# Input projection with convolution and FoX columns first, RWKV columns last, and the recurrence beside the sample's past attention

## The chip, the cores and the metric

The kernel runs on one core of a Trainium2 chip. The metric is the device time of one execution in microseconds (us); of several executions the median is taken. The core has five instruction streams that run in order, each on its own: TensorE (PE, with its weight loads as a row of its own, PEld), VectorE (DVE), ScalarE (ACT), GpSimd (POOL) and SyncE (SP). They wait for each other by semaphores. DMAs are issued from the streams of SP, ACT and POOL, and 16 DMA engines carry them.

## The reference

One inference step of one layer of a hybrid decoder, for a prompt of 512 tokens and for 8 samples of 4 new tokens each, so 544 token columns in all. All arithmetic is float32. Cut to what matters here:

```python
z = rms_norm(x, g_mix) @ w_in               # (544, 1024) @ (1024, 3080)
za, zb, zc = split(z, [1024, 1024 + 1544])  # RWKV | FoX | convolution columns
# RWKV-7: token shift, gates (decay w, a, g), then a recurrence over tokens per head
sa = einsum('bhvk,bhk->bhv', S, -kk_t)
S  = S * w_t + sa[..., None] * (kk_t * a_t) + v_t[..., None] * k_t
# FoX: q, k normed per head, log-sigmoid forget gate, causal attention in the prompt;
# each sample attends to 2048 past tokens from a paged cache and to its own 4
kp = cache_fox_k[l][page_table]; vp = cache_fox_v[l][page_table]
s_past = einsum('bqhd,bkhd->bhqk', q, kp) * scale + cT[..., :, None] + exT[..., None, :]
# convolution: u = a * sigmoid(b), causal depthwise convolution of width 31, layer norm, silu
x = x + concat([ya, yb, yc]) @ w_out
x = x + cross_attend(x, mk, mv, ...)        # mk, mv = projections of 256 memory tokens
x = x + conv_ffn(x, ...)
```

The outputs are x and all new cache rows and states. The past of the samples is 8 x 16 pages of 128 tokens in each of the K and V caches, 67 MB together, which have to be gathered by page number.

## The kernel before

A large product keeps float32 accuracy by splitting both operands: w = w_hi + w_lo and x = x_h + x_l, and taking three passes (`gemm_steps`). For a block of 128 weight columns, ACT casts w_hi from the loaded `w_raw`, DVE subtracts to get w_lo, and PE takes 8 row blocks x 3 passes x 2 spans of token columns = 48 matmuls into a bank `bank_g`, of which there are two. The bank is then evacuated by DVE (`evac_z`, `evac_conv`, `evac_fl`, `evac_fox`). The weights of two blocks are loaded at a time into a ring of two 1 MB buffers called `w_raw`.

The program is written for a tile scheduler: Python generators give their work in steps, `weave` and `woven` take from several of them in proportion to a rate, and the scheduler then fixes the order on each engine, with `urgent` and `high_priority` as its priorities. Nothing is reordered at run time. The part of the program up to the first residual is this:

- **Start.** The tokens are loaded, transposed and split into `act_h` and `act_l` (`xh`, `xl`); the forget-gate sums of the past (`LF`, `LT`, `later`, `NX`) are made.
- **RWKV columns.** 8 blocks of `w_in` (`order_z`), each followed by the token shift (`evac_z`), with the gates (`gates`) made as soon as the blocks that they need are there.
- **FoX and convolution columns beside the recurrence.** `fox_and_conv` takes one block of forget gates (`evac_fl`), 4 of the convolution (`evac_conv`) and 12 of FoX (`evac_fox`, then `fox_block` with norm, transposes and the stores of the new rows). Woven with it are `rwkv_recurrence` (`inverses`, then per pair of chunks `chain`, `stateless` and `stateful`, then `sample_steps` for the samples) and `conv_ahead`, whose `conv_taps` are the 31 taps as multiply-adds of DVE on tiles `four`, with POOL and ACT taking a fifth of the taps.
- **Past attention of the samples beside the rest.** `sample_past` does for each of the 8 samples 4 gathers of K (1 MB each, into the ring `w_raw`, transposed on DVE into `KT`, then products in `bank_s`), a softmax, 4 gathers of V (into the ring `page` of three, products in `bank_v`) and closing steps in `bank_k`. Gathers are issued by POOL (`four_pages`). Beside it runs `rest`: the attention of the prompt (`attend`, in the three banks `bank_r`), the memory norm and the convolution's layer norm (`side_work`), the projections of the memory (`memory`, products of `xT` in `bank_g`), and the output projection with its residual (`out_prompt`, products of `four` in `bank_g`); `out_sample` closes.

The stage after that begins with the cross attention's query projection, whose products are called `bank_d`, and goes on to the feed-forward network; its code is not touched. The line that sets the last stage's rates is

```python
weave((urgent(sample_past(), 0), 135.0), (rest(), 148.0, 0.06))
```

Of the kernel before, what the change touches and what calls it, by code (L numbers as in the profile page):

```python
# [8 lines left out]
F32 = mybir.dt.float32  # L9
# [145 lines left out]
def hybrid_step(tc, A):  # L155
# [375 lines left out]

    rp = ExitStack()
# [9 lines left out]
    f1s = ExitStack()  # L542
    f1 = pool("f1a", 1, f1s)
    reset = f1.tile([128, NT], F32, name="tap")
    load(out=bf, in_=A["fox_b_f"].rearrange("l h -> h l"))
    nc.scalar.dma_start(out=reset, in_=A["cf"][:, -NT:])
    nc.gpsimd.memset(zb[:, :, 0:1], 0.0)
# [135 lines left out]
    for p4, po in enumerate(QUAD):  # L683
        vts(out=kidx[po], in0=ptb[po, p4::4], scalar1=32, scalar2=CU("lane").bitcast(I32)[po], op0=MUL, op1=ADD)
# [10 lines left out]


    f2 = pool("f2a", 2, f1s)
    nc.vector.memset(e8.bitcast(F32), 0.0)
    nc.gpsimd.memset(cum.bitcast(F32), 0.0)
    for po in QUAD:  # L700
        acopy(e8[po.start: po.start + 8], ident[0:8, 0:8])
    nc.vector.memset(cpad, 0.0)
    nc.gpsimd.memset(U[:, :, : CW - 1], 0.0)
    now, after = {}, []

    def finish(n=1):

        for x in after:
            x[0] -= n
        while after and after[0][0] <= 0:  # L710
            after.pop(0)[1]()

    def evac_fl(ps, i, a):

        if a == 0:
            now["y"] = f2.tile([128, NT], F32, name="fraw")[:8]
        y = now["y"]
        with tc.high_priority():
            vtt(out=halves(y)[a], in0=ps[:8], in1=halves(rs)[a][:8], op=MUL)
        if a == 0:  # L720
            return
        vts(out=y, in0=y, scalar1=bf, scalar2=None, op0=ADD)
        logf = f2.tile([128, NT], F32, name="fsq")[:8]
        e = f2.tile([128, NT], F32, name="ft")[:8]
        act(out=e, in_=y, func=AF.Abs)
        act(out=e, in_=e, func=AF.Exp, scale=-1.0)
        act(out=e, in_=e, func=AF.Ln, bias=ones[:8, 0:1])
        vstt(out=logf, in0=y, scalar=0.0, in1=e, op0=MINO, op1=SUB)
        ccum = f2.tile([128, NT], F32, name="ft")[:8]
        nc.vector.tensor_tensor_scan(out=ccum[:, :SEQ], data0=ones[:8, 0:1].broadcast_to([8, SEQ]), data1=logf[:, :SEQ],  # L730
                                     initial=0.0, op0=MUL, op1=ADD)
        nc.vector.tensor_tensor_scan(out=cpad[:8], data0=C("reset_s")[:8], data1=logf[:, SEQ:],
                                     initial=0.0, op0=MUL, op1=ADD)
        for ro in HALF:
            acopy(cum[ro][:8], ccum[:, :SEQ])
            vtt(out=cum[ro][32:40], in0=ccum[:, :SEQ], in1=cum[0:8].bitcast(F32), op=SUB)
        after.append([6, lambda: fl_rows(logf)])

    def fl_rows(logf):
        ps = xb()  # L740
        for i in range(4):
            tr(ps[:, i * 8: i * 8 + 8], logf[:, i * 128: (i + 1) * 128])
        tr(ps[:NS, 32:40], logf[:, SEQ:])
        lt = f1.tile([128, 40], F32, name="lt")
        vcp(lt[:, :32], ps[:, :32])
        vcp(lt[:NS, 32:], ps[:NS, 32:40])
        store(out=A["p_fox_logf"][0, 0].rearrange("(i p) h -> p i h", p=128), in_=lt[:, :32].rearrange("p (i h) -> p i h", h=8))
        store(out=A["s_fox_logf"][0].rearrange("b t h -> (b t) h"), in_=lt[:NS, 32:])

    def tok_major(dst, dst_s, src, src_s):  # L750

        ps = xb()
        for i in range(4):
            tr(ps[:, i * 128: (i + 1) * 128], src[:, i * 128: (i + 1) * 128])
        anycp(dst, ps.rearrange("p (i c) -> p i c", c=128))
        ps = xb()
        tr(ps[:NS, :128], src_s)
        vcp(dst_s, ps[:NS, :128])

    def evac_fox(ps, i, a):  # L760
        j, kind = i // 3, i % 3
        if a == 0:
            now["raw"] = f2.tile([128, NT], F32, name="fraw")
            if kind < 2:
                now["sq"] = f2.tile([128, NT], F32, name="fsq")
        raw, sq = now["raw"], now.get("sq")
        with tc.high_priority():
            vtt(out=halves(raw)[a], in0=ps, in1=halves(rs)[a], op=MUL)
            if kind < 2:
                act(out=halves(sq)[a], in_=halves(raw)[a], func=AF.Square)  # L770
        finish()
        if a:
            after.append([1, lambda: fox_block(j, kind, raw, sq)])

    def fox_block(j, kind, raw, sq):
        c = slice(j * 128, (j + 1) * 128)
        if kind == 2:
            tok_major(vF[:, :, c], vs[:NS, c], raw[:, :SEQ], raw[:, SEQ:])
            store(out=A["s_fox_v"][0].rearrange("b t h d -> (b t) (h d)")[:, c], in_=vs[:NS, c])
            store(out=A["p_fox_v"][0, 0].rearrange("(i p) h d -> p i (h d)", p=128)[:, :, c], in_=vF[:, :, c])  # L780
            return
        t = f2.tile([128, NT], F32, name="ft")
        sums = []
        for (lo, n) in EVEN:
            ps2 = xb()
            mm(ps2[:, :n], bones, sq[:, lo: lo + n])
            act(out=sq[:, lo: lo + n], in_=ps2[:, :n], func=AF.Ln, scale=1.0 / 64, bias=eps_rms)
            sums.append(ps2[:, :n])
        act(out=sq, in_=sq, func=AF.Exp, scale=-0.5)
        for h in range(2):  # L790
            half_xyy(halves(t)[h], halves(sq)[h], sums[h], 1.0 / 64, EPS_RMS)
        vstt(out=raw, in0=raw, scalar=nkg if kind else qg, in1=sq, op0=MUL, op1=MUL)
        dst, dst_s = ((yF[:, j, :SEQ], qsT[:, j]), (kF[:, j], ksT[:, j]))[kind]
        vstt(out=dst, in0=t[:, :SEQ], scalar=1.5, in1=raw[:, :SEQ], op0=SUB, op1=MUL)
        vstt(out=dst_s, in0=t[:, SEQ:], scalar=1.5, in1=raw[:, SEQ:], op0=SUB, op1=MUL)
        if kind:
# [6 lines left out]
    def evac_conv(ps, i, a):  # L803
        m = i // 2
        finish()
        if i % 2 == 0:
            if a == 0:
                now["a"] = f2.tile([128, NT], F32, name="fraw")
# [1390 lines left out]
```

## Time and profile before

| | |
|---|---|
| median of 3 runs | 1257.33 us (1253.19 to 1261.47) |
| profiled execution | 1253.36 us, of which the span of the trace is 1251.6 us |
| busy PE, PEld, DVE, ACT, POOL | 1162.3, 998.9, 810.1, 499.6, 290.0 us |
| mean granted TensorE clock | 0.965 of full speed |
| DMA | 173.83 MB, mean 139 GB/s |

The span is counted from the first instruction of the trace. Busy time of an engine is the union of its instructions' spans; a matmul's span includes its way through the array, so several overlap and a busy PE need not be at its peak. Idle time is put down to what ended it. A window's row gives its start and end, its length, the busy time of each engine with the number of its instructions (PE, PEld, DVE, ACT and POOL; for a single tile PE, PEld, DVE and ACT, as far as they touch it), then the granted TensorE clock as a share of full speed, the busy share of the DMA engines and what they moved in GB/s. A group's row gives line, engine, operation, output<-input and shapes, the count, and behind the bar the busy time in us, the mean of one in ns, and the idle time just before with what ended it. In the chain and in a timeline the first two numbers are start and length.

### The profile page before, as it was taken

The page shows a single profiled execution, that of the slowest core. Times are in us where ns is not written, and L with a number is a line of the kernel's source. Part 1 is how long each engine was busy: PE and PEld are TensorE (multiplying, and loading weights), DVE is VectorE, ACT ScalarE, POOL GpSimd, SP SyncE. Part 2 cuts the span into 40 slices and gives each one's busy share as a digit, 9 for nine tenths or more (in the row PEclk, how much of TensorE's full clock was granted, in tenths as well). Part 3 has the DMA queues.
Part 4 walks back from the last instruction along what each step waited for, and adds up shares of the span by engine and source line. Part 5 has one row for each costly group of instructions (what it writes and reads, how often), then busy time and mean ns, then how long its engine had stood idle before and what let it go on. Part 6 is the DMA issues. An engine that isn't in the chain of part 4 may idle for free.

```text
span 1251.6 us, 24835 instructions
## 1 busy us (share of the span) xinstructions
PE 1162.3 (93%) x10410; PEld 998.9 (80%) x10410; DVE 810.1 (65%) x1516; ACT 499.6 (40%) x994; POOL 290.0 (23%) x322
## 2 busy tenths in 40 slices
PE   6899989999988998988989979999999999999997
PEld 6788878895654566765478756999999999999996
DVE  4699998865578667772355766567777325767522
ACT  5354453351346554423343233254444223444321
POOL 1253340113533323212322330031111001111120
PEclk9999999998689999989999999999999999999998
DMA  7222220131578799988435361232322332322241
GB/s 236 61 60 51 62 78 2 54 89 44 161 287 323 281 350 360 339 266 277 169 114 160 118 251 59 77 121 70 100 90 59 97 91 95 102 90 70 81 125 36
DMA packets 129649, 173.83 MB, mean 139 GB/s; under 512 B 7029, under 2 KB 110981, under 8 KB 121336
## 3 DMA queue, kind: packets, MB, share of 16 engines
q1 hardware_dynamic: 88160, 70.76, 18.7%
q0 software_dynamic: 15216, 84.80, 18.4%
q10 hardware_dynamic: 26160, 16.66, 4.7%
q8 instruction: 82, 1.34, 0.4%
q14 instruction: 31, 0.25, 0.1%
HBM read 164.54 MB, written 7.88 MB: 138 GB/s over the span
## 4 chain that ended last, share of the span: by engine, by line
PE 65%; DVE 12%; issue 9%; DMA 6%; ACT 5%; POOL 2%; SPq 0%; POOLq 0%; ACTq 0%; DVEq 0%
PE bank_g L186 39%; PE bank_r L186 8%; PE bank_d L186 7%; PE bank_s L186 3%; DMA page<-in_cache_fox_v_dram,kidx 3%; PE bank_a L186 2%; PE bank_v L186 2%; DMA w_raw<-in_cache_fox_k_dram,kidx 2%; DVE KT L1404 2%; DVE w_lo L247 2%; PE bank_r L216 1%; PE bank_t L216 1%; DMA x_tok<-in_x_prompt_dram 1%; PE bank_x L216 1%; ACT w_lo L1440 1%
## 5 line engine op out<-in xcount | busy, mean ns | idle before, releaser
L186 PE MATMUL bank_g<-four,w_hi 128*128 128x272 f32 (+1 forms) x1536 | 277.5, 299 | 5.7 <-ACT w_hi L177 5.0
L177 ACT CAST w_hi<-w_raw 128x1024 fp32r<-128x1024 f32 (+3 forms) x149 | 140.4, 945 | 259.5 <-PE bank_g L186 187.9
L186 PEld LDWEIGHTS bank_g<-four,w_hi 128*128 128x128 f32 x1536 | 221.9, 188 | 15.2 <-ACT w_hi L177 5.3
L247 DVE TENSOR_TENSOR w_lo<-w_raw,w_hi 128x1024 fp32r<-128x1024 f32 (+3 forms) x149 | 163.4, 1098 | 82.4 <-ACT w_hi L177 75.3
L186 PE MATMUL bank_g<-four,w_lo 128*128 128x272 f32 (+1 forms) x768 | 171.8, 299 | 0.0
L186 PE MATMUL bank_g<-act_h,w_hi 128*128 128x272 f32 (+2 forms) x400 | 124.6, 311 | 6.1 <-ACT w_hi L177 2.5
L186 PEld LDWEIGHTS bank_g<-four,w_lo 128*128 128x128 f32 x768 | 122.0, 189 | 5.9 <-issue 3.4
L186 PE MATMUL bank_g<-act_h,w_lo 128*128 128x272 f32 (+2 forms) x400 | 122.5, 307 | 0.0
L186 PE MATMUL bank_g<-act_l,w_hi 128*128 128x272 f32 (+2 forms) x400 | 121.6, 304 | 0.0
L2110 POOL TENSOR_SCALAR ysm<-HS,vec 128x32 f32<-128x32 f32 x44 | 42.0, 954 | 255.1 <-ACT HS L177 255.1
L186 PEld LDWEIGHTS bank_g<-act_h,w_hi 128*128 128x128 f32 x400 | 79.0, 198 | 10.5 <-ACT w_hi L177 2.9
L186 PEld LDWEIGHTS bank_g<-act_h,w_lo 128*128 128x128 f32 x400 | 78.9, 197 | 2.8 <-issue 1.2
L1404 DVE STREAM_TRANSPOSE KT<-w_raw 128x2048 f32<-128x2048 f32 x32 | 73.5, 2301 | 11.7 <-DMA w_raw<-in_cache_fox_k_dram,kidx 10.7
L186 PEld LDWEIGHTS bank_g<-act_l,w_hi 128*128 128x128 f32 x400 | 79.0, 198 | 2.4 <-issue 1.1
L186 PE MATMUL bank_d<-four,w_hi 128*128 128x272 f32 x384 | 78.2, 299 | 0.0
L186 PE MATMUL bank_g<-in_h,w_hi 128*128 128x272 f32 x352 | 73.5, 290 | 0.0
L186 PE MATMUL bank_g<-in_l,w_hi 128*128 128x272 f32 x352 | 73.5, 290 | 0.0
L186 PE MATMUL bank_g<-in_h,w_lo 128*128 128x272 f32 x352 | 73.2, 289 | 0.0
L186 PEld LDWEIGHTS bank_d<-four,w_hi 128*128 128x128 f32 x384 | 61.7, 192 | 1.0
L2102 DVE TENSOR_TENSOR up<-bank_g,tot 128x544 f32<-128x544 f32 x44 | 31.8, 722 | 44.6 <-PE bank_g L186 44.6
L1389 POOL DMA_INDIRECT w_raw<-in_cache_fox_k_dram,kidx x32 | 36.0, 1125 | 94.2 <-DVE KT L1404 62.6
L186 PE MATMUL bank_d<-four,w_lo 128*128 128x272 f32 x192 | 56.7, 295 | 0.0
(632 smaller groups left out, 2439.3 us busy)
## 6 DMA issues: line engine op xcount, KB each, us to landing
w_raw<-in_w_up_dram SPq DMA_DIRECT2D x20, 1024.0 KB, 5.1
w_raw<-in_w_down_dram SPq DMA_DIRECT2D x16, 704.0 KB, 4.5
w_raw<-in_w_in_dram SPq DMA_DIRECT2D x17, 512.0 KB, 4.6
w_raw<-in_cache_mem_k_dram SPq DMA_DIRECT2D x16, 512.0 KB, 5.0
sV<-in_cache_mem_v_dram POOLq DMA_DIRECT2D x12, 512.0 KB, 6.0
w_raw<-in_w_in_dram SPq DMA_DIRECT2D x4, 1024.0 KB, 7.1
w_raw<-in_w_xk_dram ACTq DMA_DIRECT2D x8, 512.0 KB, 12.4
w_raw<-in_w_xv_dram ACTq DMA_DIRECT2D x8, 512.0 KB, 5.1
```

The costliest lines, as they stand in the source:

```text
L177: nc.scalar.copy(out, in_)
L186: pinned(nc.tensor.matmul(out, lhsT, rhs, start=start, stop=stop, skip_group_check=True))
L216: pinned(nc.tensor.transpose(out=out, in_=in_, identity=ident[p0:p0 + k, p0:p0 + k]))
L247: tt(out=l, in0=src, in1=h.bitcast(F32), op=SUB)
L1389: nc.gpsimd.indirect_dma_start(out=t, out_offset=None, in_=A[cache][0].rearrange("n (k j) h d -> (n k) (j h d)", j=4), in_offset=bass.Indi ...
L1404: nc.vector.transpose(out=KT, in_=K)
L1440: anycp(PT[to, j].rearrange("p (g h q) -> p g h q", g=4, q=TS), ps[po].rearrange("p (g h a q) -> p a g h q", g=4, a=4, q=TS)[:, p4])
L2102: vtt(out=two(x[:, 2:]), in0=ev2(ps), in1=two(rstd), op=MUL)
L2110: nc.gpsimd.tensor_scalar(out=ysm, in0=H[:, 2:6, 1:], scalar1=w[2], scalar2=b, op0=MUL, op1=ADD)
```

## The change

Three things are moved, and no arithmetic is added or taken away.

1. The order of the columns of `w_in`. The convolution's 4 blocks are taken first (the preloaded first weights are theirs), then the forget gate and the 12 FoX blocks, woven with `conv_ahead` at rates 106 and 60, and RWKV's 8 blocks last, woven with what is left of `conv_ahead`. The convolution's blocks take spans of 256 and 288 columns now.
2. The recurrence is no longer woven with the projection. It is the first thing in `rest`, so it runs beside `sample_past`; the rate of `rest` goes from 148 to 215, and its head start from 0.06 to 0.03.
3. Pools follow: the FoX pool `f2a` is closed before the RWKV pool `rt` opens, `reset` has a tile of its own, the gather indices `kidx` are made before the RWKV columns, and the pool `cv` is opened only after the recurrence.

```diff
@@ start
-            early = weights(A["w_in"][0], 8, [m * 128 for m in order_z[:2]])
+            early = weights(A["w_in"][0], 8, [COL_CONV, COL_CONV + 256])
...
@@ the block from "f1s, f2s = ExitStack(), ExitStack()" to conv_ahead is moved ahead of the RWKV block, with
+    EARLY = ((0, 256), (256, 288))
+
     def fox_and_conv():
         x = blocks(xh), blocks(xl)
+        yield from gemm_steps(w_in, [COL_CONV + (2 * half + m) * 128 for m in range(2) for half in range(2)], *x, evac_conv, gb,
+                              spans=EARLY, first=early)
+        conv_done[0] = True
         yield from gemm_steps(w_in, [COL_FL], *x, evac_fl, gb)
         for j in range(4):
-            if j == 0:
-                yield from gemm_steps(w_in, [COL_CONV + (2 * half + m) * 128 for m in range(2) for half in range(2)], *x, evac_conv, gb)
-                conv_done[0] = True
             yield from gemm_steps(w_in, [COL_FOX + kind * 512 + j * 128 for kind in range(3)], *x, lambda ps, i, a, j=j: evac_fox(ps, 3 * j + i, a), gb)
         finish(9)
...
+    conv_work = conv_ahead()
+    weave((fox_and_conv(), 106.0), (conv_work, 60.0, 0), first=True)
+    f2s.close()
...
@@ RWKV columns
-    blocks_done, after_r1 = [0], gates()
-    need = next(after_r1)
-    for step in gemm_steps(w_in, [m * 128 for m in order_z], blocks(xh), blocks(xl), evac_z, gb, spans=((0, 256), (256, 288)), first=early):
-        if need is not None and blocks_done[0] >= need:
-            need = next(after_r1, None)
-    for _ in after_r1:
-        pass
+    blocks_done = [0]
+
+    def rwkv_columns():
+        after_r1 = gates()
+        need = next(after_r1)
+        for step in gemm_steps(w_in, [m * 128 for m in order_z], blocks(xh), blocks(xl), evac_z, gb, spans=EARLY):
+            if need is not None and blocks_done[0] >= need:
+                need = next(after_r1, None)
+            yield step
+        for _ in after_r1:
+            pass
+
+    weave((rwkv_columns(), 44.0), (conv_work, 30.0))
...
@@ after the projection
-    recurrence, conv_work = urgent(rwkv_recurrence(), 800), conv_ahead()
-    weave((fox_and_conv(), 106.0), (recurrence, 79.0, 0), (conv_work, 84.0, 0), first=True)
+    recurrence = urgent(rwkv_recurrence(), 800)
...
@@ rest
-        yield from woven((recurrence, 48.0), (conv_work, 48.0))
+        yield from recurrence
         recurrence_end()
...
-    weave((urgent(sample_past(), 0), 135.0), (rest(), 148.0, 0.06))
+    weave((urgent(sample_past(), 0), 135.0), (rest(), 215.0, 0.03))
```

How the order on the engines moves is shown at three places. The first is DVE inside the recurrence's `inverses`, where a small triangular solve goes over 15 steps (`Dr`, then `X`). Before, between its steps stand convolution taps (`four<-U,vec,four`), FoX norms (`ft`, `fraw`) and evacuations:

```order
L955 TENSOR_REDUCE X<-Dr 128x12
L226 SCALAR_TENSOR_TENSOR ft<-bank_x,ft 128x272
L954 TENSOR_TENSOR Dr<-X,zbuf_1206 128x13x13
L794 SCALAR_TENSOR_TENSOR four<-ft,fraw 128x512
L955 TENSOR_REDUCE X<-Dr 128x13
L795 SCALAR_TENSOR_TENSOR qsT<-ft,fraw 128x32
L855 SCALAR_TENSOR_TENSOR four<-U,vec,four 128x512
L768 TENSOR_TENSOR fraw<-bank_g,rs 128x272
L954 TENSOR_TENSOR Dr<-X,zbuf_1206 128x14x14
```

Now, on the same engine in the same solve, transposes of K pages (`KT<-w_raw`) and a sample's softmax (`st`, `Pn`) stand there:

```order
L1416 STREAM_TRANSPOSE KT<-w_raw 128x2048
L968 TENSOR_TENSOR Dr<-X,zbuf_2653 128x11x11
L1435 ISA tq,st<-tq,cf 128x32
L1435 ISA st 128x1
L969 TENSOR_REDUCE X<-Dr 128x11
L1437 RECIPROCAL st<-st 128x1
L968 TENSOR_TENSOR Dr<-X,zbuf_2653 128x12x12
L1439 TENSOR_SCALAR Pn<-Pn,st 128x4
L969 TENSOR_REDUCE X<-Dr 128x12
L1416 STREAM_TRANSPOSE KT<-w_raw 128x2048
```

What fills the gaps of the recurrence on DVE has gone from work whose inputs lie on the chip to transposes that wait for a gather. All 32 K transposes now stand ahead of the last step of the recurrence (`recurrence_end`), the first two of them ahead of `inverses`; of the 32 gathers of V, 19 are issued before it and 13 after.

The second place is PE in the output projection. Before, its products (`bank_g<-four`) alternate with transposes of x and with the last samples' K products:

```order
L186 MATMUL bank_g<-four,w_hi 128x512
L186 MATMUL bank_s<-KT,w_hi 32x128 x32
L216 MATMUL bank_r_6116<-ident,w_raw 128x32 x4
L216 MATMUL bank_r_6122<-ident,w_raw 128x32 x4
L186 MATMUL bank_g<-four,w_hi 128x512
L186 MATMUL bank_g<-four,w_lo 128x512
L186 MATMUL bank_g<-four,w_hi 128x512 x2
L186 MATMUL bank_g<-four,w_lo 128x512
L186 MATMUL bank_g<-four,w_hi 128x512
L186 MATMUL bank_s<-KT,w_hi 32x128 x16
```

Now the memory's and the output's products stand almost alone, as here in the memory's projection on PE:

```order
L186 MATMUL bank_g<-xT_4302,w_hi 128x256
L186 MATMUL bank_g<-xT_4303,w_hi 128x256
L186 MATMUL bank_g<-xT_4302,w_lo 128x256
L186 MATMUL bank_g<-xT_4302,w_hi 128x256
L186 MATMUL bank_g<-xT_4303,w_hi 128x256
L186 MATMUL bank_g<-xT_4302,w_lo 128x256
```

Behind the start of the memory's projection PE has no K product of a sample left, and of V only 16 products and the closing steps.

The third place is SP's queue at the start of the RWKV columns, where the samples' shift state is loaded into the tile `dp`. Now that load stands behind the weights of RWKV's third pair of blocks and waits for six semaphores of POOL's DMA queue (DMASW):

```order
L273 DMA w_raw<-in_w_in_dram 128x8x256 [waits DMAHW4_49,DVE_49]
L273 DMA w_raw<-in_w_in_dram 128x8x256 [waits DMAHW5_49,DVE_49]
L766 DMA dp<-in_state_rwkv_shift_dram 8x512 [waits DMASW2_49,DMASW5_49,DMASW1_49,DMASW6_49,DMASW0_49,DMASW7_49,DVE_49,Activation_49]
L766 DMA dp<-in_state_rwkv_shift_dram 8x512 [waits PE_49]
L273 DMA w_raw<-in_w_in_dram 128x8x256 [waits DMAHW6_49,DVE_49]
```

Before, it waited for no store:

```order
L550 DMA gup<-in_rwkv_g_up_dram 128x256 [waits DMAHW5_49]
L273 DMA w_raw<-in_w_in_dram 128x8x256 [waits DMAHW6_49,DMAHW1_49,DVE_49]
L554 DMA dp<-in_state_rwkv_shift_dram 8x512 [waits DVE_49,DMAHW0_49,PE_49,Activation_49]
L554 DMA dp<-in_state_rwkv_shift_dram 8x512
L273 DMA w_raw<-in_w_in_dram 128x8x128 [waits DMAHW2_49,DVE_49]
```

The load has moved behind the stores of the last FoX rows, whose memory its tile takes over; PE's transposes of `dp` stand among the matmuls of RWKV's second block.

## Rows read from the trace of the kernel before

**Rows 1.** Windows of the whole core

```profile
113.00:320.00 207.00, 199.49 (x2218) 164.05 (x2218) 162.08 (x366) 81.53 (x172) 50.62 (x57) 0.95 0.19 52
320.00:645.00 325.00, 286.77 (x2669) 195.56 (x2667) 210.97 (x404) 145.67 (x356) 97.74 (x90) 0.94 0.78 273
```

**Rows 2.** The same view, shorter windows

```profile
0.00:64.00 64.00, 49.26 (x322) 44.77 (x323) 35.13 (x84) 31.02 (x61) 13.16 (x30) 0.97 0.46 145
64.00:320.00 256.00, 244.05 (x2518) 205.18 (x2517) 210.16 (x432) 105.23 (x203) 74.16 (x76) 0.95 0.20 55
80.00:100.00 20.00, 17.02 (x116) 16.32 (x115) 19.90 (x26) 9.14 (x15) 14.42 (x10) 0.91 0.31 81
120.00:180.00 60.00, 53.25 (x406) 48.93 (x407) 57.21 (x116) 32.23 (x53) 25.47 (x28) 0.97 0.28 73
300.00:320.00 20.00, 20.00 (x62) 9.82 (x62) 5.93 (x19) 2.68 (x8) 1.88 (x2) 0.57 0.11 27
320.00:340.00 20.00, 17.32 (x127) 11.83 (x125) 14.81 (x28) 7.32 (x21) 12.93 (x13) 0.67 0.55 174
323.00:454.00 131.00, 115.41 (x1218) 70.26 (x1216) 96.56 (x201) 70.83 (x206) 49.39 (x50) 0.91 0.79 291
```

**Rows 3.** The chain that ended last: start us, us, what

```profile
46.03 3.40 DMA dp<-in_state_rwkv_shift_dram
338.69 7.58 DMA w_raw<-in_cache_fox_k_dram,kidx
646.93 4.61 PE bank_d L186 x24
```

**Rows 4.** Groups of instructions by line, PE, 13:64

```profile
L186 PE MATMUL bank_g<-act_h,w_hi 128*128 128x256 f32 (+1 forms) x78 | 24.6, 315 | 2.5 <-ACT w_hi L177 2.5
```

**Rows 5.** The same view, DVE, 113:320

```profile
L855 DVE SCALAR_TENSOR_TENSOR four<-U,vec,four 128x512 f32<-128x512 f32 x48 | 38.7, 806 | 0.4
...
L954 DVE TENSOR_TENSOR Dr<-X,zbuf 128x1 f32<-128x1 f32 (+14 forms) x15 | 9.0, 600 | 0.0
...
L1006 DVE COPY_PREDICATED zsb<-cu,bank_r 128x32 f32<-128x32 uint32 x1 | 0.2, 182 | 0.0
```

**Rows 6.** Windows of tile bank_g: PE, PEld, DVE, ACT busy (count), PEclk, DMA, GB/s

```profile
13.00:323.00 310.00, 188.06 (x1200) 165.39 (x1200) 23.11 (x57) 0.00 (x0) 0.96 0.23 63
454.00:540.00 86.00, 54.21 (x384) 50.03 (x384) 6.52 (x16) 2.89 (x8) 0.96 0.97 339
540.00:645.00 105.00, 54.28 (x192) 35.48 (x192) 5.53 (x8) 0.00 (x0) 0.95 0.62 206
```

**Rows 7.** DMA issues, 113:320: KB each, median us from issue to landing

```profile
out_dram<-tok POOLq DMA_DIRECT2D x3, 256.0 KB, 4.5
```

**Rows 8.** Windows of tile bank_r, columns as in rows 6

```profile
113.00:320.00 207.00, 89.41 (x1464) 61.84 (x1463) 35.49 (x99) 18.21 (x47) 0.95 0.19 52
323.00:454.00 131.00, 63.71 (x336) 37.90 (x334) 25.06 (x51) 15.68 (x37) 0.91 0.79 291
```

**Rows 9.** Windows of tile bank_s, then of bank_v

```profile
320.00:645.00 325.00, 51.55 (x1104) 36.02 (x1104) 5.50 (x8) 0.59 (x1) 0.94 0.78 273
...
323.00:454.00 131.00, 20.83 (x128) 5.83 (x128) 0.00 (x0) 1.76 (x3) 0.91 0.79 291
```

**Rows 10.** Groups by line, DVE, 323:454

```profile
L1404 DVE STREAM_TRANSPOSE KT<-w_raw 128x2048 f32<-128x2048 f32 x20 | 45.9, 2298 | 1.1 <-DMA w_raw<-in_cache_fox_k_dram,kidx 1.1
```

**Rows 11.** Timeline of DVE: start us, us, what

```profile
332.96 4.50 DVE L1404 STREAM_TRANSPOSE KT<-w_raw 128x2048 f32<-128x2048 f32 x2
```

**Rows 12.** Tile w_raw on POOL, 330:560: issues' durations in ns, first and last; landing

```profile
L1389 POOL DMA_INDIRECT w_raw<-in_cache_fox_k_dram,kidx x30: 999/1006/2062, 338.7 to 543.7; - x30
...
DMA to landing us min/median/max: 5.5/7.9/11.8
```

**Rows 13.** Timeline of PE at the output projection's first and last products

```profile
550.93 0.80 PE L186 MATMUL bank_g<-four,w_hi 128*128 128x512 f32 x1 [5.05 <-ACT w_hi L177]
...
634.74 0.40 PE L186 MATMUL bank_g<-four,w_lo 128*128 128x512 f32 x1
```

More of the change, by code (lines that the diff above doesn't have):

```diff
@@ L529, in hybrid_step, with finish @@
     gls.close()
+    f1s, f2s = ExitStack(), ExitStack()
+    f1 = pool("f1a", 1, f1s)
+    f2 = pool("f2a", 2, f2s)
+    load(out=bf, in_=A["fox_b_f"].rearrange("l h -> h l"))
+    nc.vector.memset(e8.bitcast(F32), 0.0)
+    nc.gpsimd.memset(cum.bitcast(F32), 0.0)
+    for po in QUAD:
+        acopy(e8[po.start: po.start + 8], ident[0:8, 0:8])
+    nc.vector.memset(cpad, 0.0)
+    nc.gpsimd.memset(U[:, :, : CW - 1], 0.0)
+    now, after = {}, []
+    def finish(n=1):
+        for x in after:
+            x[0] -= n
+        while after and after[0][0] <= 0:
+            after.pop(0)[1]()
@@ new lines, in fl_rows @@
+    def fl_rows(logf):
+        ps = xb()
+        for i in range(4):
+            tr(ps[:, i * 8: i * 8 + 8], logf[:, i * 128: (i + 1) * 128])
+        tr(ps[:NS, 32:40], logf[:, SEQ:])
+        lt = f1.tile([128, 40], F32, name="lt")
+        vcp(lt[:, :32], ps[:, :32])
+        vcp(lt[:NS, 32:], ps[:NS, 32:40])
+        store(out=A["p_fox_logf"][0, 0].rearrange("(i p) h -> p i h", p=128), in_=lt[:, :32].rearrange("p (i h) -> p i h", h=8))
+        store(out=A["s_fox_logf"][0].rearrange("b t h -> (b t) h"), in_=lt[:NS, 32:])
@@ new lines, in tok_major, with evac_fox @@
+    def tok_major(dst, dst_s, src, src_s):
+        ps = xb()
+        for i in range(4):
+            tr(ps[:, i * 128: (i + 1) * 128], src[:, i * 128: (i + 1) * 128])
+        anycp(dst, ps.rearrange("p (i c) -> p i c", c=128))
+        ps = xb()
+        tr(ps[:NS, :128], src_s)
+        vcp(dst_s, ps[:NS, :128])
+    def evac_fox(ps, i, a):
+        j, kind = i // 3, i % 3
+        if a == 0:
+            now["raw"] = f2.tile([128, NT], F32, name="fraw")
+            if kind < 2:
+                now["sq"] = f2.tile([128, NT], F32, name="fsq")
+        raw, sq = now["raw"], now.get("sq")
+        with tc.high_priority():
+            vtt(out=halves(raw)[a], in0=ps, in1=halves(rs)[a], op=MUL)
+            if kind < 2:
+                act(out=halves(sq)[a], in_=halves(raw)[a], func=AF.Square)
+        finish()
+        if a:
+            after.append([1, lambda: fox_block(j, kind, raw, sq)])
@@ L694, in hybrid_step @@
     rp.close()
[L697 to L796, printed above, removed]
-            tokm = f2.tile([128, 4, 128], F32, name="tok", bufs=1)
-            rows = f2.tile([NS, 128], F32, name="krow", bufs=1)
-            tok_major(tokm, rows, dst, dst_s)
-            store(out=A["p_fox_k"][0, 0].rearrange("(i p) h d -> p i (h d)", p=128)[:, :, c], in_=tokm)
-            store(out=A["s_fox_k"][0].rearrange("b t h d -> (b t) (h d)")[:, c], in_=rows)
```

228 lines of the change are left out of this document (139 added, 89 removed).

## Prediction

> **What bounds the kernel now.** I read the windows by stage first: in each, which engine is full, and what it is full of. In the woven stage PE is busy 199.49 of 207 us and DVE 162.08 [rows 1], so neither looks free; but a matmul's span includes its way through the array, and waits of one product for another count as busy. The dense stretches tell more: DVE reaches 19.90 of 20 and 57.21 of 60 us [rows 2]. So where projection, convolution taps and FoX norms meet, DVE is the bound, and PE follows. The end of this stage is different: from 300 to 320 DVE is busy 5.93 of 20 us, PE finishes 62 instructions, and the granted TensorE clock is 0.57 [rows 2]. The recurrence has run dry of filler there, one product waits for the last, and the clock has gone down: (1 - 0.57) x 2 x 20 = 17 us of it at 1.2 instead of 2.4 GHz.
>
> From 323 on the bound is another. The chain goes by gathers of K [rows 3], the DMA engines are 0.79 busy [rows 2], and DVE is at 211 of 325 us [rows 1]. Each K page needs a landing in the ring of two `w_raw`, then a transpose of 2.30 us [rows 10] that empties it. In 454 to 540 the DMA share is 0.97 [rows 6]: the memory's projection shares its weight loads with the gathers.
>
> So the program has a DVE-bound stage with idle DMA (0.19, [rows 1]) and a DMA-bound stage with idle engines. The change lays the recurrence, which needs little DMA, beside the gathers. The section that it touches ends where the cross attention's projection starts, at 646.93 [rows 3]. I sum it anew up to there and leave the rest as it is.
>
> **The change part by part.**
>
> *Start and convolution columns.* By 64 us 232 matmuls of the projection had run (78 + 77 + 77; one of the three rows stands in [rows 4]), a stall for the shift's load included (46.03, 3.40 us, [rows 3]). Now the first 4 blocks and the forget gate's are 240, without that stall: **60 us**.
>
> *The rest of the projection, with all taps and norms.* From 64 to 320 DVE has 210.16 us [rows 2]; what of FoX still came behind 320 I estimate at 10 of the 14.81 us of 320 to 340 [rows 2]. The recurrence's part goes out: in 113 to 320, 47 of the view's 76 groups, from `Dr` with 9.0 us down to 0.2 [rows 5], are its own, 73.9 us of the 182.8 that all groups add up to (their spans overlap), so of the 162.08 us of busy time 65.5. What stays is 210.2 + 10 - 65.5 = 155. At a density of 0.975 (between 57.21/60 and 19.90/20) that is **159 us**. PE's part is 20 blocks x 48 matmuls at 0.141 (54.21/384) to 0.157 (188.06/1200) [rows 6], 135 to 151 us, and some 15 of transposes and small products: just hidden beneath DVE, and not by much.
>
> *The shift's load.* It waits now for stores of the last FoX rows. A store of `tok` took 4.5 us to land [rows 7] and the load 3.40 [rows 3]; PE has a transpose of it among the matmuls of RWKV's second block, so PE's queue stands behind it. The stores may long have landed (bound 0), or nothing covers them (7.9). The weave ends its FoX part just before, so I take **8**.
>
> *The recurrence with the gathers.* All 32 K transposes stand before its last step, the first two ahead of it: 30 pages, and 19 V pages. Four candidates for the bound. DVE: 65.5 of the recurrence, 32 x 2.30 = 73.5 of transposes, and 15 for the softmax of 7 samples, about 155. PE: the recurrence's 89.41 (17 of it at half clock) and 51.55 for K's products, and 19 of 32 V pages, about 30: 165 to 170, [rows 8, 9], of which much is waiting. DMA: 49 MiB at the 339 GB/s of the fullest window [rows 6], 152. The ring: landing 7.9 and transpose 2.3 [rows 10, 12] for two buffers, 5.1 a page, 153. All four stand at 152 to 170, and that is just why none will be met: three rings with queues in fixed order lose at each other. The nearest row of such a mixture is the attention stage: 20 transposes between 332.96 and 454 [rows 10, 11], 6.05 us a page, with DVE at 96.56 of 131 and DMA at 0.79 [rows 2]. At that pace 30 pages are 182, and 6 for the first landing (5.5 at least, [rows 12]): **188 us**. The bounds are 155 and, below, 232.
>
> *Prompt attention with 13 V pages.* Before, `bank_r` held PE for 63.71 us, beside K [rows 8]; 14 V pages cost 20.83 [rows 9]. **84 us**; the gathers themselves, 13.6 MB at 291 GB/s, are 47 and lie beneath.
>
> *Memory's projection.* No gather is left beside it; `bank_g` needs 54.21 us for its 384 matmuls [rows 6] in 86 us of window. **54 us**.
>
> *Head of the output projection.* Its first product waited 5.05 us for ACT's casts [rows 13], and the step before it needs some 3: **8**.
>
> *Output projection.* 192 matmuls held 54.28 us between other work [rows 6]; at the tempo of its last rows, 2 x 0.23 us for 512 columns each, 45. I take **48**.
>
> *Tail.* From its last product, 634.74, to `bank_d`, 646.93 [rows 3, 13]: **12**.
>
> Sum: 60 + 159 + 8 + 188 + 84 + 54 + 8 + 48 + 12 = 621 us, against 646.9: 26 us off the profiled execution's 1253.4, so 1227.5. The median of the runs lies 4 us above the profiled one, half of which I take as belonging to it: **1230 us**.
>
> One rule speaks against this. Gathers are issued by POOL, whose issue took 1.0 us in the median and 2.06 at most [rows 12]; in 323 to 454 DVE was busy three quarters of the time.
>
> The Trainium skill ("SBUF — State Buffer", section "Who interferes with whom") says that VectorE and GpSimd share one pair of ports under an exclusive lock, and that GpSimd can't write the descriptors of a DMA while VectorE holds it. The one stretched issue in the row could be that, and no row shows what it would be beside a VectorE that is never idle. By it each gather would come later, as in the slower case below.
>
> **The rivals.**
>
> *K does not limit.* If landings come down, since the memory's weights no longer share the DMA engines, the stage goes at DVE's 155 + 5 = 160 us, 28 less: 1202. For it: landing at least was 5.5 [rows 12], which gives (5.5 + 2.3)/2 = 3.9 a page. Against it: the median of 7.9 with V beside it, as will be again.
>
> The Trainium skill ("DMA: Bandwidth & Descriptors", section "Anatomy of one DMA — SWDGE (gpsimd) path") fits 2.0 us plus the bytes by 436 GB/s: 4.4 us for a page, an estimate by which K would never limit. The trace disagrees, with 7.9 [rows 12].
>
> *The recurrence's own chain decides.* While it ran before, DVE was idle for 207 - 162.08 = 45 us with all that filler at hand [rows 1], and PE fell to 0.57 clock at its end. If this idle time is the recurrence's latency and comes on top, with the filler now waiting for gathers (some 15 us more), the stage takes 155 + 45 + 15 = 215, 27 more, and the change only moves the bubble: 1257.
>
> *Gathers slow down.* If they land at the worst of the rows, 11.8, with an issue of 1.0 before and the transpose of 2.3 behind [rows 10, 12], a page takes 15.1/2 = 7.55 and the stage 30 x 7.55 + 6 = 232: 44 us more, 1274, slower than before. It decides from a page of (188 + 26 - 6)/30 = 6.9 us. For it: from 338.7 to 543.7 the K issues came at 205/29 = 7.07 us each [rows 12], though other stages set that pace; and transposes standing in the middle of the recurrence's solve make it wait for each gather, DVE being in order. Against it: the gathers have more slack ahead than in the memory's stage.
>
> **How the numbers follow.** Forecast 0.50, with its own range of 1211 to 1249 (the stage at 170 to 205, the shift's bubble 0 to 8); K not limiting 0.13, at 1202; the chain 0.22, at 1257; slow gathers 0.15, at 1274. The measurement can tell about 1%, so 1244.8 to 1269.9 is the same. The range 1196 to 1266 leaves out half of the slow gathers and the outer parts of the others. Faster: 0.13, and 0.46 of the forecast's 0.50, and 0.06 of the chain: 0.65. Slower: 0.12 of the slow gathers and 0.02 of the chain. Same is the rest, 0.21.
>
> **What would show it.** In the new trace: the last FoX block's evacuation at about 165 us and the last projection matmul near 225; a gap of PE in RWKV's second block ended by `dp`'s load; K transposes at 6 us each between 225 and 410; DMA share at about 0.8 there; the memory's 384 matmuls in 54 us; `bank_d` at 621. I am wrong in the split if DVE in the FoX stage is not dense; wrong in the whole if the K transposes are spaced by 7 us or more, or if DVE's idle time in the recurrence is ended by PE's small products and not by gathers. A TensorE clock near 0.6 through the recurrence, as in 300 to 320, would take the memory's and the attention's stage with it only if it lasted into them, which 323 to 454 with 0.91 [rows 2] speaks against.

## The result, and the profile after

The changed kernel is slower: 1328.1 us in the median of four runs (1325.5 to 1332.4) against 1256.1 (1253.2 to 1261.5), a ratio of 1.0571 with a 95% interval of 1.0525 to 1.0618. The forecast was 1230, so both the sign and the size were wrong. The profiled execution has a span of 1330.7 us.

The timeline of PE in the changed kernel gives the borders of the stages (start, length, what, idle before):

```profile
40.27 0.61 PE L186 MATMUL bank_g<-act_h,w_hi 128*128 128x288 f32 x1 [5.88 <-DVE fraw L653]
...
245.52 0.29 PE L186 MATMUL bank_g<-act_l,w_hi 128*128 128x288 f32 x1
...
486.18 0.45 PE L186 MATMUL bank_r<-cum,e 40*128 40x128 f32 x1
...
581.66 0.50 PE L186 MATMUL bank_g<-xT,w_hi 128*128 128x256 f32 x2 [1.74 <-ACT w_hi L177]
...
659.36 1.22 PE L186 MATMUL bank_g<-four,w_hi 128*128 128x512 f32 x2 [3.68 <-ACT w_hi L177]
...
726.61 0.80 PE L186 MATMUL bank_d<-four,w_hi 128*128 128x272 f32 x2
```

The second block of the projection starts at 40, the last projection products stand at 246, the prompt attention begins at 486 (`cum,e`), the memory's projection at 582, the output's products run steadily from 659, and `bank_d`, which stood at 646.93 [rows 3], begins at 726.6. All of the loss lies ahead of it. The windows of these stages answer to [rows 1] (columns as there):

```profile
0.00:67.00 67.00, 49.77 (x313) 45.73 (x314) 36.58 (x77) 35.09 (x66) 13.34 (x21) 0.90 0.46 131
67.00:246.00 179.00, 156.82 (x1087) 147.85 (x1087) 147.88 (x231) 79.34 (x131) 65.14 (x69) 0.93 0.26 77
246.00:486.00 240.00, 190.29 (x2736) 114.36 (x2736) 157.51 (x356) 65.97 (x209) 71.70 (x79) 0.86 0.65 229
486.00:582.00 96.00, 86.65 (x533) 44.13 (x533) 48.20 (x141) 49.48 (x131) 18.46 (x18) 0.97 0.56 187
582.00:648.00 66.00, 59.79 (x449) 54.95 (x448) 42.28 (x77) 28.55 (x48) 1.21 (x1) 0.92 0.51 152
648.00:727.00 79.00, 64.35 (x400) 51.56 (x399) 34.27 (x51) 22.22 (x35) 14.44 (x13) 0.89 0.29 86
```

The third row is the one to look at: the recurrence beside the samples takes 240 us, and no engine is full in it. DVE is busy 157.5 and idle 82.5, and the DMA engines are 0.65 busy. Who ended DVE's idle time there is told by its waits (engine and line, what it waited for, us in total, times, longest):

```profile
DVE KT L1416 <- DMA w_raw<-in_cache_fox_k_dram,kidx: 14.9, 6, 7.4
DVE S L1078 <- PE bank_r L186: 9.6, 2, 6.8
DVE w_hi L1311 <- PE bank_s L186: 9.2, 4, 3.4
DVE zbuf L1125 <- PE bank_r L186: 5.9, 4, 2.3
```

Gathers end 14.9 us of it, in six waits. PE ends some 51 us, in many short waits for the recurrence's own products and the samples' (these four rows are the longest). How the two are mixed shows in DVE's timeline inside a pair of chunks:

```profile
356.87 0.36 DVE L1117 COPY_PREDICATED zbuf<-cu,inv 128x128 f32<-128x128 uint32 x1
357.25 0.23 DVE L1480 TENSOR_REDUCE ysm<-bank_k 64x16 f32<-64x64 f32 x1
357.51 2.31 DVE L1416 STREAM_TRANSPOSE KT<-w_raw 128x2048 f32<-128x2048 f32 x1
359.85 0.30 DVE L1125 COPY_PREDICATED zbuf<-cu,bank_r 128x128 f32<-128x128 uint32 x1
360.18 0.43 DVE L1210 TENSOR_TENSOR zb<-bank_r,zb 64x256 f32<-64x256 f32 x1
360.64 0.38 DVE L1117 COPY_PREDICATED zbuf<-cu,inv 128x128 f32<-128x128 uint32 x1
...
363.81 2.30 DVE L1416 STREAM_TRANSPOSE KT<-w_raw 128x2048 f32<-128x2048 f32 x1
366.04 0.38 DVE L1210 TENSOR_TENSOR zb<-bank_r,zb 64x256 f32<-64x256 f32 x1
```

Behind 28 of the 31 transposes in this stage DVE goes on with no wait, mostly with a step of the recurrence: by then that step was ready, and it had stood behind up to 2.3 us of somebody else's work. (The 32nd transpose stands at 490, just behind the stage.)

### The profile page after: what moved, and what is told of

Same layout as the page of the kernel before. It is cut to its first block, busy times and chain, and to the rows that moved or that the text cites. A ratio compares the mean times of both kernels' runs of the same rounds, so it can differ in the third digit from the quotient of the medians.

```text
span 1330.7 us, 24845 instructions
## 1 busy us (share of the span) xinstructions
PE 1189.7 (89%) x10410; PEld 1011.7 (76%) x10410; DVE 817.2 (61%) x1519; ACT 497.3 (37%) x991; POOL 286.7 (22%) x322
## 4 chain that ended last, share of the span: by engine, by line
PE 59%; DMA 7%; issue 6%; DVE 3%; ACT 3%; POOL 1%; POOLq 0%; ACTq 0%; SPq 0%; DVEq 0%
PE bank_g L186 34%; PE bank_r L186 7%; PE bank_d L186 6%; DMA page<-in_cache_fox_v_dram,kidx 5%; PE bank_s L186 3%; PE bank_v L186 3%; PE bank_a L186 2%; PE bank_r L216 1%; DMA w_raw<-in_cache_fox_k_dram,kidx 1%; PE bank_t L216 1%; DVE KT L1416 1%; DMA w_raw<-in_w_out_dram 1%; ACT w_lo L1452 1%; ACT w_hi L177 1%; DMA w_raw<-in_cache_mem_k_dram 0%
## 5 line engine op out<-in xcount | busy, mean ns | idle before, releaser
L1416 DVE STREAM_TRANSPOSE KT<-w_raw 128x2048 f32<-128x2048 f32 x32 | 73.6, 2301 | 21.1 <-DMA w_raw<-in_cache_fox_k_dram,kidx 14.9
L186 PE MATMUL bank_v<-page,w_lo 128*32 128x512 f32 x256 | 63.1, 670 | 13.7 <-DMA page<-in_cache_fox_v_dram,kidx 11.6
L186 PE MATMUL bank_s<-KT,w_hi 128*32 128x128 f32 x1024 | 59.1, 326 | 18.1 <-DVE KT L1416 16.3
L1401 POOL DMA_INDIRECT page<-in_cache_fox_v_dram,kidx x32 | 32.8, 1026 | 161.6 <-PE bank_v L186 125.6
L186 PEld LDWEIGHTS bank_s<-KT,w_hi 128*32 128x32 f32 x1024 | 38.7, 129 | 37.3 <-issue 16.9
```

The lines of the kernel that those rows point to most:

```text
L186: pinned(nc.tensor.matmul(out, lhsT, rhs, start=start, stop=stop, skip_group_check=True))
L1401: nc.gpsimd.indirect_dma_start(out=t, out_offset=None, in_=A[cache][0].rearrange("n (k j) h d -> (n k) (j h d)", j=4), in_offset=bass.Indi ...
L1416: nc.vector.transpose(out=KT, in_=K)
```

## The experiments

"Stage" is the time from the last projection matmul to the first `cum,e`. Runs 13 and 14 were executed four times each, the others once; the kernel before spread from 1249.9 to 1264.4 us beside the later ones, so differences of a few us in a whole say little. Two theories stood first. A: gathers and their waits stretch it. B: the recurrence is a long chain by itself. C, that the samples' instructions stretch a short chain, came with the second four runs, and D, an account of the whole loss, with the third.

**1. The recurrence ahead of the last stage.**

```diff
+    for _ in recurrence:
+        pass
-    weave((urgent(sample_past(), 0), 135.0), (rest(), 215.0, 0.03))
+    weave((urgent(sample_past(), 0), 135.0), (rest(), 148.0, 0.06))
```

> The changed kernel with the recurrence run by itself between the projection and the samples (nothing beside it), the last stage at the old rates 148 and 0.06. In the changed kernel 240 us lie between the last projection matmul (246) and the prompt attention's first product (486). Theory A (the gathers and their waits stretch the stage): the recurrence alone is short, 100 to 120 us, near its 65.5 us of VectorE and 89 us of TensorE, and the whole is 246 + 110 + 324 (what the samples and the rest took before) + 604 = about 1284 us, faster than the changed kernel. Theory B (the recurrence's own chain of small steps is long, whatever stands beside it): alone it takes 180 us or more, and the whole is 1360 us or more.

Measured: 1344.5 us, stage 243. It settles nothing: the scheduler put K gathers and transposes between the recurrence's steps again, since they were ready.

**2 to 4. Gathers left out.** Run 2 keeps two K pages for everything, run 3 two K pages for the transposes alone, run 4 a loaded tile for V's products (with one buffer of the `page` ring less, to make room).

```diff
-            K = four_pages(wraw.tile([128, 2048], F32, name="w_raw"), "cache_fox_k", b, pg)
+            K = kept[pg % 2] if len(kept) > 1 else four_pages(wraw.tile([128, 2048], F32, name="w_raw"), "cache_fox_k", b, pg)
+            if len(kept) < 2:
+                kept.append(K)
...
-            t = four_pages(page(), "cache_fox_v", b, pg)
+            t = kept[pg % 2]
```

> The changed kernel with only two K pages gathered; all transposes and all V products read these two pages again, so 30 K and all 32 V gathers and the waits for them are left out (the past scores and values are of wrong pages). Theory A: the stage of 240 us falls to VectorE's 155 to TensorE's 170 us, the whole to about 1255. Theory B: the stage stays at 215 us or more, the whole at 1300 or more.

> The changed kernel with only two K pages gathered, read again by all transposes; V is gathered as before. Theory A with K's landing as the limit: stage 175 to 190 us, whole about 1270. Theory A with V's gathers and the POOL queue as the limit: stage above 215. Theory B: stage above 215.

> The changed kernel with no V gather: V's products read a tile that is loaded once; K is gathered as before. If V's place in POOL's queue (its issue waits for the products of the page three before, and K's issue stands behind it) is what spaces the K pages, the stage falls to 185 us and the whole to about 1270. If K's landing spaces them, or the recurrence's own chain, the stage stays at 225 or more.

Measured: 1303.8, 1327.9 and 1303.2 us; stages 230, 256 and 240. Theory A falls: with 62 of 64 gathers gone the stage is 10 us shorter. V's place in POOL's queue isn't it either. Why run 3's stage is 16 us longer than the changed kernel's is open. What V's gathers do cost lies later: without them (run 4) the attention took 81 us, the memory 63, and the way from there to `bank_d` 70, against 95, 66 and 79.

**5. The recurrence alone in truth.** As run 1, its rates too, and the page numbers of the gathers get an operand from the recurrence's last rows, times zero.

```diff
+    for _ in recurrence:
+        pass
+    vstt(out=kidx, in0=ynT[:, 0, SEQ:], scalar=0.0, in1=kidx, op0=MUL, op1=ADD)
```

> As the first run, but the samples' page numbers are made to depend on the recurrence's result, so that no gather and none of the samples' past work can stand in it. With nearly all gathers left out the stage of 240 us had only gone to 230, so the gathers are not what fills it. Theory B (the recurrence's chain of small dependent steps is long by itself): from the last projection matmul to its sample steps 180 us or more. Theory C (the chain is short, 110 to 140 us, and is stretched by the samples' instructions that stand between its steps on VectorE and TensorE): 140 us or less. The whole under B about 1390, under C about 1330.

Measured: 1327.2 us, stage 149, between what B and C asked for. The whole is that of the changed kernel, so on balance putting the samples beside the recurrence had hidden nothing. The windows of its stage, and of run 8's, 2's and 11's (below), one fence for each:

```profile
241.00:390.00 149.00, 106.36 (x1547) 75.36 (x1546) 73.04 (x224) 26.97 (x75) 14.83 (x24) 0.75 0.08 22
```
```profile
245.00:422.00 177.00, 164.59 (x2669) 102.46 (x2668) 94.75 (x318) 56.91 (x172) 21.09 (x30) 0.95 0.07 20
```
```profile
247.00:477.00 230.00, 200.34 (x2899) 120.14 (x2898) 158.75 (x374) 71.31 (x220) 22.03 (x31) 0.89 0.08 22
```
```profile
248.00:477.00 229.00, 158.99 (x1762) 88.06 (x1760) 163.37 (x394) 76.97 (x237) 21.31 (x30) 0.75 0.12 35
```

Take DVE's busy time from the length: 76 us idle alone, then 82, 71 and 66, and 82 in the changed kernel. DVE's work more than doubles, and the idle time hardly falls. In run 3 it is even 95 us:

```profile
247.00:502.00 255.00, 203.20 (x2845) 119.09 (x2843) 160.16 (x373) 70.28 (x219) 43.11 (x51) 0.85 0.34 115
```

Alone, 63 of DVE's 76 us of idle time are waits for the chain's own products in `bank_r`, of which these are the longest:

```profile
DVE beta L1178 <- PE bank_r L186: 11.9, 4, 4.0
DVE S L1078 <- PE bank_r L186: 11.1, 2, 8.3
```

**6. The old column order, recurrence beside the samples.**

```diff
-    weave((fox_and_conv(), 106.0), (recurrence, 79.0, 0), (conv_work, 84.0, 0), first=True)
+    weave((fox_and_conv(), 106.0), (conv_work, 84.0, 0))
...
-        yield from woven((recurrence, 48.0), (conv_work, 48.0))
+        yield from recurrence
```

> The kernel before with its column order (RWKV first, FoX and convolution after), but the recurrence taken out of the FoX stage and put beside the samples as in the change (rates 215 and 0.03, the convolution's pool opened after it). If it is the recurrence's place that costs: the FoX stage falls from 207 us to 155 to 170, the stage beside the samples is 230 to 245, and the whole is 1300 to 1330. If the column order costs (late RWKV, late gates, the shift's load, the start): the whole is 1275 or less.

Measured: 1289.8 us, but the scheduler had put the recurrence back beside the FoX columns (113 to 315), so it says nothing of its place. What it lost lies behind: from the first `cum,e` to `bank_d` it took 364 us against 324, at the new rates. Run 9 makes the move a true one.

**7. The recurrence first.** `urgent(rwkv_recurrence(), 800)` becomes 4000.

> The changed kernel with the recurrence's priority raised from 800 to 4000 steps ahead, so that its ready steps go before nearly all of the samples'. Theory C: the recurrence's part falls below 200 us and the whole by 20 us or more. Theory B: no change beyond 10 us.

Measured: 1319.1 us, stage 235. B's outcome; at a higher priority the transposes still stand in the chain.

**8. Also without transposes.** As run 2, and `KT` is transposed for the first two pages alone.

> The run without gathers, and also without 30 of the 32 K transposes (the products read the two transposed pages again): some 69 us of VectorE taken out of the stage of 230 us. Theory C: the stage falls by 40 us or more, to 190 or less. Theory B: by less than 15.

Measured: 1256.5 us, stage 177. C's outcome: 53 us against run 2 for 30 transposes of 2.3 us, so 1.8 us each. The whole fell by 47, so 6 of the 53 came back behind the stage.

**9 and 10. The old order with a true move.** Two small instructions bind the recurrence to the last FoX block:

```diff
+    for j in range(2):
+        vstt(out=beta[:, j, :SEQ], in0=vF[:, 3], scalar=0.0, in1=beta[:, j, :SEQ], op0=MUL, op1=ADD)
```

Run 9 has the edit of run 6 with it, run 10 the edit of run 5 besides.

> The kernel before with its column order, the recurrence beside the samples as in the change (215 and 0.03); one operand of the recurrence is made to depend on the last FoX block's rows, so that it can't slip back beside the FoX columns (two small VectorE instructions more). Theory D (the recurrence is a chain of 149 us alone, of which VectorE idles 76; beside FoX and the taps it cost only 323 - 246 = 77 us, beside the samples it costs its whole length, so the change loses 149 - 77 = 72): 1320 to 1335 us, as the changed kernel. If the new column order has a share in the loss: below 1310.

> The same, but the samples' page numbers depend on the recurrence's result, so that the recurrence stands alone between projection and samples, last stage at 148 and 0.06. Theory D: projection done at about 246 to 250, recurrence 149 us, the rest 324: the kernel before plus 72, about 1328 us, no slower than with the samples beside it. If the samples' work really hides beneath the recurrence: 30 us or more above the run before this one.

Measured: 1308.6 and 1310.6 us. Projection done at 229 and 232, stages 229 and 140; their windows:

```profile
229.00:458.00 229.00, 187.92 (x2656) 111.85 (x2656) 147.56 (x339) 63.30 (x198) 67.64 (x71) 0.81 0.64 229
```
```profile
232.00:372.00 140.00, 100.74 (x1544) 70.78 (x1545) 69.42 (x219) 28.21 (x78) 12.86 (x18) 0.76 0.10 28
```

Again the samples beside it hide nothing (2 us). And D is right on the place but not on its being everything: of the 72 us, 52 go with the recurrence's place and 20 with the new column order (by single runs).

**11. Without the samples' products.** As run 2, and K's products and three quarters of V's are left out on PE.

> The run without gathers (stage 230 us), and also without the K products and three quarters of the past V products on TensorE; all 32 transposes stay on VectorE. If the transposes in VectorE's fixed order are what lengthens the chain, each by its own time: the stage stays at 205 us or more. If the samples' products on TensorE hold the chain up: 185 or less.

Measured: 1297.8 us, stage 229. PE is busy 41 us less, and the stage doesn't move, so it isn't PE's load that holds the chain up. One thing works against this reading: the granted clock fell too, from 0.89 to 0.75, and the recurrence's own products (tile `bank_r`) held PE for 99.1 us instead of run 2's 91.7 (104.4 in run 5, 87.3 in run 8). So by an estimate from these 7 us the products cost the stage some 8 us and not 1, and of run 8's 53 us some 4 are the clock's.

**12, 15 and 16. Transposes in quarters**, in the changed kernel, in run 9's, and in the changed kernel at 148 and 0.06:

```diff
-            nc.vector.transpose(out=KT, in_=K)
+            for n in range(4):
+                nc.vector.transpose(out=KT[:, 512 * n: 512 * n + 512], in_=K[:, 512 * n: 512 * n + 512])
```

> The changed kernel with each K transpose of 128 x 2048 cut into four of 128 x 512, one after the other. If a transpose of 2.3 us harms because the chain's next step has to wait for its end, quarters let it in sooner and the stage falls by 15 us or more. If every us of VectorE that is put between the chain's steps adds itself, the stage is 240 plus the cost of four starts each (about 0.4 us x 30), 245 to 255.

> The old column order with the recurrence beside the samples (1308.6 us, stage 229) and K transposes in quarters. If the quarters' gain in the stage (36 us in the new order) is real and is given back later only by the place of the V gathers: stage 195 to 205 us, and the rest behind it, 245 us before, longer by 20 or more; whole 1290 to 1305. If it was a chance of the new order: stage 225 or more.

> The changed kernel with quarters and the old rates of the last stage, 148 and 0.06, so that the samples stand further ahead of the rest. In the run with quarters at 215 the stage was 204 us, but the loads of the memory's and the output's weights took 14.9 and 17.0 us behind V gathers. If these collisions give the gain back: fewer V gathers behind the memory's start, memory and output 20 us shorter, whole about 1300. If the samples' V work is what is left over at any rate: within 8 us of 1323.

Measured: 1323.1, 1293.8 and 1319.3 us; stages 204, 201 and 215. I first took the 36 us of run 12 for the gain of shorter pieces. The groups of DVE in the stages of 12 and 15 say otherwise:

```profile
L1417 DVE STREAM_TRANSPOSE KT<-w_raw 128x512 f32<-128x512 f32 x96 | 63.9, 689 | 8.2 <-PE bank_s L186 6.5 <-DMA w_raw<-in_cache_fox_k_dram,kidx 1.6
```
```profile
L1408 DVE STREAM_TRANSPOSE KT<-w_raw 128x512 f32<-128x512 f32 x82 | 55.6, 692 | 8.9 <-DMA w_raw<-in_cache_fox_k_dram,kidx 5.4 <-PE bank_r L186 3.3
```

96 quarters are 24 pages, 82 are 20.5, where the changed kernel and run 9 have these in their stages:

```profile
L1416 DVE STREAM_TRANSPOSE KT<-w_raw 128x2048 f32<-128x2048 f32 x31 | 71.3, 2301 | 16.0 <-DMA w_raw<-in_cache_fox_k_dram,kidx 14.9 <-PE bank_r L186 0.9
```
```profile
L1407 DVE STREAM_TRANSPOSE KT<-w_raw 128x2048 f32<-128x2048 f32 x30 | 69.0, 2302 | 13.6 <-DMA w_raw<-in_cache_fox_k_dram,kidx 11.8 <-PE bank_r L186 0.9 <-PE bank_s L186 0.8
```

So much of the gain is pages pushed behind the stage. Over the length of the recurrence alone (149 us in the new order, 140 in the old), a page costs (240 - 149)/31 = 2.9 us in the changed kernel, (229 - 140)/30 = 3.0 in run 9, (201 - 140)/20.5 = 3.0 in run 15, (215 - 149)/22.75 = 2.9 in run 16, and 2.3 in run 12 alone. (This is the stage's growth by the number of pages, with softmax, products and gathers in it.) In run 12 the 7 pages explain some 20 of the 36 us; the rest is open. Of the 36, 28 and 25 us that the three stages fell, 30, 14 and 15 came back between the stage and `bank_d`. Run 15's stage and whole lie in the ranges expected for a real gain, but much of it by pages that moved; run 16 came out on the side on which V's work is left over at any rate. In run 12 the chain behind the stage shows a load of memory weights at 547.62 that took 14.94 us and one of output weights at 627.02 that took 17.04.

**13. The FoX pools opened first.** In the changed kernel PE's second block waits until 40 (first row above). DVE's timeline of the changed kernel shows what stands ahead of the first bank's evacuation, `fraw`:

```profile
31.87 5.40 DVE L523 TENSOR_TENSOR_SCAN later<-cf,later,bank_x 64x512 f32<-64x512 f32 x4 [2.63 <-PE bank_x L216]
37.31 2.45 DVE L528 COPY NX<-later 32x512 f32<-32x512 f32 x4
39.79 0.42 DVE L653 SCALAR_TENSOR_TENSOR fraw<-bank_g,rs 128x256 f32<-128x256 f32 x1
```

```diff
+    f1s, f2s = ExitStack(), ExitStack()
+    f1 = pool("f1a", 1, f1s)
+    f2 = pool("f2a", 2, f2s)
     gls = ExitStack()
     gl = pool("gl", 1, gls)
...
-    f1s, f2s = ExitStack(), ExitStack()
-    f1 = pool("f1a", 1, f1s)
-    f2 = pool("f2a", 2, f2s)
```

> The changed kernel with the FoX pools opened ahead of the pool in which the forget-gate sums of the past are made, so that the first block's evacuation needn't wait for memory that these sums still hold (in the changed kernel the first bank is emptied at 40 us, behind four scans and the copies of NX; in the kernel before at 25). If that is the new column order's loss at the start: the second block starts at 26 instead of 40, the projection ends 10 to 15 us sooner, and the whole is 8 to 15 us shorter than the changed kernel, about 1315. If VectorE's taps and norms bound the projection anyhow, the gain is gone by its end: within 4 us of 1328.

Measured: 1322.1 us, ratio to the kernel before 1.050 (1.044 to 1.056). DVE and PE then:

```profile
26.55 0.42 DVE L653 SCALAR_TENSOR_TENSOR fraw<-bank_g,rs 128x256 f32<-128x256 f32 x1
...
27.69 0.40 PE L186 MATMUL bank_g<-act_h,w_hi 128*128 128x288 f32 x1
```

12 us are won at the start, and 6 are left at the projection's end (240.0 for 246.4) and in the whole, between what the two sides asked for. The wait was for memory: in the old order the first evacuation goes into `zb`, which has its own.

**14. The kernel before in quarters.**

> The kernel before, with nothing moved, but its K transposes cut into quarters. If long VectorE instructions hold up the prompt attention beside them as they hold up the recurrence: 5 to 15 us faster than before. If that stage goes by the gathers, as its chain says: within 1% (the 0.4 us that quarters cost more a page is hidden).

Measured: 1276.0 us, ratio 1.013 (1.006 to 1.020): a little slower, which neither side had. The stage from 321 to the memory's first product, 131 us before, took 147. Why is open, and with it what quarters are worth: single runs 12, 15 and 16 were 5, 15 and 9 us faster with them (16 with other rates too), this one 19 us slower. No run that computes everything beat the kernel before.

## Why the prediction was wrong

**The step that failed** is *the recurrence with the gathers*. It bounded the stage by four throughputs, 152 to 170 us, and took 188 by the pace of K pages beside attention. The recurrence's own length, 149 us, was not among the four, and DVE's idle time in it was taken as room for the transposes. Measured 240, 52 us over. DVE's work was right, 155 summed and 157.5 measured; its idle time was not, 33 us left by the forecast and 82.5 measured. The runs lay the stage out in steps: 149 alone (run 5), 177 with the samples but without 30 transposes and the gathers (run 8), 230 with the transposes (run 2), 240 with the gathers. Taking out the products hardly changes it (run 11). The 28 us of the first step are the samples' other work; no run takes it apart.

So work put between the steps adds most of its time (53 us of stage for 69 us of transposes), and DVE's idle time stays at 66 to 95 us, whatever was added. Why can be argued in part: alone, DVE's 76 us come as gaps between steps, the order on DVE is fixed ahead, and a transpose put there begins when it is its turn, not when DVE is free. The waits bear this out as far as they go: those for the chain's own `bank_r` fell from 63 us alone to 36 in the changed kernel, and in their place came waits for gathers (14.9), for the samples' products and for the softmax on ACT. That the fixed order is the reason was not tested by an order that fits the gaps better; the higher priority of run 7 won 9 us.

**The gain of the step before it was over-read.** I took the recurrence out of the FoX stage for its 65.5 us of DVE. Beside FoX it cost 323 - 229 = 94 us, and alone it takes 140 (runs 9, 10): there 46 of its 140 us were hidden, since taps and norms filled DVE's idle time down to 45 [rows 1]. Moving it gave that up for a place where nothing is hidden on balance. These 46 us are most of run 9's 52. The others lie in the samples' work: in run 9 it lengthens the stage by 89 us (229 for 140) and shortens the way from there to `bank_d` by 79 (245 for 324).

**The rivals.** The right mechanism was in *the recurrence's own chain decides*, chance 0.22, mis-sized: it took DVE's idle time as the 45 us that FoX's fill had left of it, where the chain alone has 76. With 76 its sum, 155 + 76 and 15 for the gathers, comes to 246; measured 240. *Gathers slow down* had nearly the number, 232 us, with the wrong reason: K issues came at (464 - 214)/31 = 8.1 us each, with the ring waiting for transposes that stood in the chain (run 2 shows that the gathers themselves cost 10 us). POOL's issues of K took 1.01 us in the median and 1.93 at most, as before [rows 12]. The lock of VectorE and GpSimd in the Trainium skill ("SBUF — State Buffer", section "Who interferes with whom") left no mark beyond that. *K does not limit* was nearly true, and gave nothing. Both signs that the prediction had named for being wrong in the whole are in the trace: the transposes came (464.1 - 252.1)/30 = 7.1 us apart, and PE ended most of DVE's idle time.

**The other terms.** Start, 67 against 60: the wait for the pool's memory, which I hadn't seen in the order (run 13). The rest of the projection with the shift's bubble, 179 against 167: DVE is busy 147.9, near the 155 that I summed, at a density of 0.83 and not 0.975. There is no bubble of the shift's load: PE's transposes of `dp` stood at 188.3 with no wait for it, and RWKV's second block took 7 us. The new order's share is 20 us by the medians and 24 by the traces of run 9 and the changed kernel. The projection ends 18 later, 6 of it by the start (run 13); the other 11 or so have no known cause, with DVE's work the same (148.4 us in the 162 from 67 on in run 9). The stage is 11 longer, 5 of it by the gates, whose end now stands bare between the projection and the recurrence's first product (246.4 to 255.0, against 228.8 to 231.9 in run 9). And 5 come back behind the stage. Attention 95.5 against 84, memory 66 against 54, and tail 21 against 12 (from 705.2 to 726.6): much of it is the 13 V pages that I had put wholly beneath attention, for without V's gathers (run 4) attention took 81 and the tail 12, though memory still 63. PE's chain in the memory's projection still stands at one:

```profile
610.47 6.86 DMA page<-in_cache_fox_v_dram,kidx
```

so "no gather is left beside it" was wrong, and the closing products of the samples, hidden before beneath the output's, now stand behind it. Head and output products were right (57 against 56). 7 + 12 + 52 + 11.5 + 12 + 1 + 9.5 = 105, and 621 + 105 = 726.

## What to carry to other kernels

A chain of small dependent steps has a length of its own, which no engine's busy time shows: measure it alone before moving it, and compare what it costs where it stands. Work that is put between its steps on an in-order engine can add most of its time, so a stage with idle engines is no proof of room; what was hidden in the old place counts as loss. And when an experiment shortens a stage, count the work in it before believing the gain.

## What was not expected of the hardware

In the recurrence alone PE was granted 0.75 of its clock over 149 us, and 0.76 over 140 in the old order, which is about half of the time at 1.2 GHz; with the samples' products beside it 0.86, without transposes between 0.95. The recurrence's own products held PE for 104 us alone, 94 beside the samples, and 87 without transposes between. So filling work gives the chain back some of its time by the clock, and still the stage grew by 2.9 us a page.
